# Correcting a list scheduler's estimate of the first weight and input transfers in a one-core Trainium2 encoder layer

## The chip, the cores and the metric

The kernel runs on one NeuronCore of a Trainium2 chip. Its engines are TensorE (PE in the profile; its weight loads are shown apart as PEld), ScalarE (ACT), VectorE (DVE), GpSimd (POOL) and SyncE (SP, which here does little but issue transfers). Each engine works through its own queue in order and waits on semaphores for what the others deliver. The metric is the device time of one execution in microseconds (us); less is better.

## The reference

One encoder layer over 512 tokens of width 1024, batch 1. The part at which the change works is the very beginning, the projection `h @ w_in`, of which the first 128 columns of keys and the first 256 of queries are computed first. `h` is x (DEPTH is 1); the lines left out put heads in shape and rotate q and k, the two mixers are attention within |i-j| <= 128 with 4 key heads and 16 query heads, and attention at three dilations, merged:

```python
    for l in range(DEPTH):
        proj = h @ w_in[l]
        qa, ka, va, qb, kb, vb = jnp.split(proj, SPLITS, axis=-1)
        ...
        o_a = windowed_gqa_sink(qa, ka, va, a_sink[l]).astype(h.dtype)
        o_b = dilated_mixture(qb, kb, vb).astype(h.dtype)
        gates = jax.nn.sigmoid(h @ w_gate[l] + b_gate[l])
        g_a, g_b = jnp.split(gates, N_BRANCH, axis=-1)
        mixed = g_a * (o_a @ w_br_a[l]) + g_b * (o_b @ w_br_b[l])
        y = mixed @ w_out[l]
        h = layer_norm(DN_ALPHA * h + y, ln1_g[l], ln1_b[l])
        f = (jax.nn.silu(h @ w_ff_gate[l]) * (h @ w_ff_up[l])) @ w_ff_down[l]
        h = layer_norm(DN_ALPHA * h + f, ln2_g[l], ln2_b[l])
```

## The kernel before

**Every product is three matmuls.** Each float32 operand is split into a rounded high part (float32r) and the rest, which the high part leaves. A product is high x high, low x high and high x low, added up in one PSUM bank. So an operand that has been loaded needs two more steps before TensorE can use it: a copy that rounds (on ACT or DVE), and a subtraction on DVE for the rest.

**The first stretch.** x lies as eight tiles of 128 x 512, one for each 128 input channels. Three weight units are multiplied with them together: `k` (the first key tile), `q` and `r` (the first and the second query tile). Each unit comes as two halves of 128 x 512 (four input channel tiles each); the first halves are cut in two pieces of 256 columns (`CUTS`, line 61), and the first piece serves x's first two tiles. `k`'s first piece is loaded over ACT's queue (line 374), everything else over SP's (lines 341 and 378). Copies are issued through line 333 (ACT) and 335 (DVE), the subtractions at lines 382 (weights) and 430 (x). The matmuls of this stretch are single operations at line 941, 72 in all: for each tile of x, nine, listed as high x high for k, q, r, then weight rest x x high for k, q, r, then weight high x x rest for k, q, r (the last two tiles go unit by unit). Ahead of it TensorE is kept busy with eight matmuls on zeros (`spin`, line 407).

**The order is written by a planner.** The kernel is built as a list of operations with dependencies, a priority, and for each engine that may do it a cost. `Program.run` (line 171) plays a clock over them: whenever an engine is free, it takes the ready operation with the best priority whose buffers fit, and that is the order in which the instructions of that engine are written into its queue. What is ready when, is the planner's own estimate. It is not a time of the chip: the chip executes the written order, whatever its own times are.

- A transfer by SP occupies SP for 0.45 (0.62 where it is small, cost up to 0.2). `dma[1]` is the time at which the transfer engines have moved all that was issued so far; a transfer adds its cost to it, 0.73 for 256 KB, and has landed 0.9 later (lines 242 to 244). One that another engine issues adds `moves` and has landed 2.0 later (lines 246 to 248). Both start from `dma = [0.0, 0.0]` (line 178).
- A result is seen by another engine after a hop of 0.20, by TensorE after 0.33, by the same engine after 0.11 (line 47).
- A copy may go to ACT or DVE. DVE takes one only if ACT isn't free within the next 0.2 (`BIAS`, line 220).
- A buffer is free again 0.20 after its last user. There are six buffers for weights on their way in (`ws`); the halves of k, q and r take all six.
- Priorities of the first operations are fixed in `FIRST` (line 62), the smaller the earlier: -1000 for k's first piece, -999.9 for x's first tile, -999.7 for q's and -999.6 for r's first piece. Constants (cosine, sine, mask, sink, identity) have about -95, the gate bias -119, the weights of the next units about -114 and more.

```python
                        if o.ready <= now and (best is None or o.prio < best.prio) and self.fits(o):
                            if e == DVE and len(o.alts) > 1 and free[ACT] < now + BIAS:
                                continue
                            best = o
```

**After it** comes the order of line 74: the next query unit `q2` (lines 454 to 456), the values `VA` (lines 627 to 629), the rotation `T`, gates `G` between the attention units `A0` to `A3` (transposes at line 675, which wait for the normalising copy at line 663), and so on to the feed-forward part, whose products are taken by a seven-product scheme (lines 1312 to 1314, 1441 to 1443).

Of the kernel before, what the change touches and what calls it, by code (L numbers as in the profile page):

```python
# [16 lines left out]
S = 512  # L17
# [28 lines left out]
PE, ACT, DVE, POOL, SP = "PE", "ACT", "DVE", "POOL", "SP"  # L46
# [11 lines left out]
D_BANK = "s"  # L58
SPIN = 4

CUTS = ((0, 256), (256, 512))
FIRST = {("k", 0): (-1000, -998.4), ("q", 0): (-999.7, -998.2), ("r", 0): (-999.6, -998.1),
         ("k", 1): (-997.7,), ("q", 1): (-997.5,), ("r", 1): (-997.4,),
# [34 lines left out]
class Program:  # L98
# [16 lines left out]
    def op(self, alts, fn, reads=(), writes=(), prio=0.0, after=(), abs_prio=None, moves=0.0):  # L115
        o = Op()
        o.urgent = self.urgent
        o.alts, o.fn = alts, fn
        o.prio = (self.T + prio if abs_prio is None else abs_prio, len(self.ops))
        o.ready, o.done, o.eng = 0.0, None, None  # L120
        deps = set(a for a in after if a is not None)
        for t in reads:
            deps.update(self.writer.get(t, ()))
        for t in writes:
            deps.update(self.writer.get(t, ()))
            deps.update(self.readers.get(t, ()))
        deps.discard(o)
        for t in reads:
            self.readers.setdefault(t, []).append(o)
        for t in writes:  # L130
            self.writer[t] = [o]
            self.readers[t] = []
        o.bufs, o.new = [], []
        o.strict, o.moves = self.strict, moves
        for t in list(reads) + list(writes):
            b = self.buf_of(t)
            if b not in o.bufs:
                o.bufs.append(b)
                b.users += 1
        o.succ = []  # L140
        o.left = len(deps)
        for d in deps:
            d.succ.append(o)
        self.ops.append(o)
        return o
# [25 lines left out]
    def run(self):  # L171
# [2 lines left out]
        pending = {e: [] for e in engines}  # L174
        times = [0.0]
        frees = []
        dma = [0.0, 0.0]

        def add(o):
            heapq.heappush(times, o.ready)  # L180
# [99 lines left out]
def dve(n, fast=False, extra=0.0):  # L280
    return 0.069 + (0.00074 if fast else 0.00104) * n + extra
# [7 lines left out]
def hybrid_layer(ctx: ExitStack, tc: tile.TileContext, wpack, xT, xtok, sink, bgate,  # L289
                 ln1g, ln1b, ln2g, ln2b, ropec, ropes, maska, maskb, identd, out):  # L290
    nc = tc.nc
# [9 lines left out]
    op = pr.op  # L301
# [7 lines left out]
    def slot(dt=F32, cls=None):  # L309
        cls = cls or "gen"  # L310
        return Buf("slot", cls, lambda: slab.tile([P, S], dt, tag="slab", bufs=N_SLOT, name=name("sl")))
# [19 lines left out]
    def copy(eng, dst, src):  # L331
        if eng == ACT:
            nc.scalar.activation(dst, src, AF.Copy)  # L333
        else:
            nc.vector.tensor_copy(dst, src)

    def f32(ap):
        return ap.bitcast(F32)
# [5 lines left out]
    def cp_alts(n, ps=False):  # L344
        return [(ACT, act(n, ps)), (DVE, dve(n, not ps))]
# [21 lines left out]
    def half_unit_by(u, j, cuts, prios):  # L367

        st, h, l = slot(F32, "ws"), slot(F32R, "whl"), slot(F32R, "whl")
        pieces[h] = pieces[l] = cuts  # L370
        for (c0, c1), ap in zip(cuts, prios):
            w = c1 - c0
            if ap == -1000:
                op([(ACT, 0.4)], lambda e, c0=c0, c1=c1: nc.scalar.dma_start(
                    st.t[:, c0:c1], wpack[u, :, j * S + c0:j * S + c1]), writes=[(st, c0)], abs_prio=ap,
                   moves=0.73 * w / S)
            else:
                op([(SP, 0.73 * w / S)], lambda e, c0=c0, c1=c1: nc.sync.dma_start(
                    st.t[:, c0:c1], wpack[u, :, j * S + c0:j * S + c1]), writes=[(st, c0)], abs_prio=ap)
            op(cp_alts(w), lambda e, c0=c0, c1=c1: copy(e, h.t[:, c0:c1], st.t[:, c0:c1]),  # L380
               reads=[(st, c0)], writes=[(h, c0), (l, "room", c0)], abs_prio=ap)
            op([(DVE, dve(w))], lambda e, c0=c0, c1=c1: nc.vector.tensor_tensor(
                l.t[:, c0:c1], st.t[:, c0:c1], f32(h.t[:, c0:c1]), op=ALU.subtract),
               reads=[(st, c0), (h, c0)], writes=[(l, c0)], abs_prio=ap)
        return h, l
# [36 lines left out]
    for j in range(2):  # L422
        for w, u in (("k", U_KA), ("q", U_QA), ("r", U_QA + 1)):
            first[w, j] = half_unit_by(u, j, ((0, S),) if j else CUTS, FIRST[w, j])
    for j in range(KD):
        st, ap = slot(F32, "xs"), FIRST["x"][j]
# [1173 lines left out]
```

## Time and profile before

| | before |
|---|---|
| median of 3 runs | 779.84 us |
| lowest and highest | 779.28, 780.75 us |
| profiled execution, whole | 779.7 us |
| its span, first to last instruction | 777.9 us |
| mean granted TensorE clock | 0.997 |
| instructions in the span | 13378 |

The profile is of one execution. Its span runs from the first to the last instruction; all instants below are counted from its start. In a row of the timeline stand start, duration, engine, line and operation, what is written and read, how many instructions are merged in the row, and in brackets how long the engine stood idle before and what ended that. A row of waits reads: who waited, for whom, total us, times, longest. A row of the windows view gives for a stretch its length, then for PE, PEld, DVE, ACT and POOL the busy time and the number of instructions, then granted clock, share of the DMA engines and GB/s. Issues of transfers are rows of "SPq" or "ACTq". Matmuls overlap: the duration of a 512-column matmul is 0.39, though one follows the other at 0.23.

### The profile page before, as it was taken

Reading aid. Unit: us, or ns where it says so; the run is one execution under the profiler, and the core shown is the slowest. Engines: PE = TensorE matmul, PEld = TensorE weight load, DVE = VectorE, ACT = ScalarE, POOL = GpSimd, SP = SyncE. Lnnn points to the kernel's source line nnn. Section 1 sums busy time; section 2 is a strip of 40 time slices with the busy share of each in tenths; the row PEclk is TensorE's granted clock in tenths of the full one; section 3 lists DMA queues with packets and bytes.
Section 4 is the critical chain, followed back from the end, with each engine's and each line's share of the span. In section 5 each row is a group of like instructions: output and inputs, shape, how many; then the busy total and the mean of one; then the engine's idle time right before and its main releaser. Section 6 shows DMA issues by size and latency. Waiting matters only on the chain.

```text
span 777.9 us, 13378 instructions
## 1 busy us (share of the span) xinstructions
PE 766.2 (99%) x4470; PEld 675.9 (87%) x4470; DVE 652.7 (84%) x1373; ACT 479.7 (62%) x1057; POOL 122.2 (16%) x288
## 2 busy tenths in 40 slices
PE   8999999999999999999999999999999999999995
PEld 6888888888888888888888899999999999999984
DVE  6378999888989898696686999797988889888697
ACT  6257785778787688693341767556655566555631
POOL 0011010101005204200020010232102331122002
PEclk9999999999999999999999999999999999999998
DMA  8745232203223224354472497699867987789102
GB/s 274 211 138 196 79 105 82 90 28 110 83 87 102 81 86 153 109 183 141 136 208 63 116 245 221 142 200 203 222 188 161 228 184 212 179 214 216 43 1 108
DMA packets 68848, 113.35 MB, mean 146 GB/s; under 512 B 8620, under 2 KB 17068, under 8 KB 68780
## 3 DMA queue, kind: packets, MB, share of 16 engines
q1 hardware_dynamic: 57116, 91.40, 36.4%
q0 software_dynamic: 11520, 20.98, 16.5%
q8 instruction: 35, 0.57, 0.3%
q14 instruction: 33, 0.27, 0.1%
q10 hardware_dynamic: 144, 0.13, 0.1%
HBM read 104.87 MB, written 4.72 MB: 141 GB/s over the span
## 4 chain that ended last, share of the span: by engine, by line
PE 96%; DVE 1%; ACT 1%; DMA 1%; issue 0%; SPq 0%; DVEq 0%; ACTq 0%
PE ps L454 10%; PE ps L455 10%; PE ps L456 10%; PE ps L1314 9%; PE ps L1313 9%; PE ps L1312 9%; PE ps L1441 4%; PE ps L1442 4%; PE ps L1443 4%; PE ps L675 3%; PE ps L1077 3%; PE ps L1079 3%; PE ps L1078 3%; PE ps L941 2%; PE ps L627 2%; PE ps L629 2%
## 5 line engine op out<-in xcount | busy, mean ns | idle before, releaser
L333 ACT ACTIVATE sl<-sl 128x512 fp32r<-128x512 f32 (+4 forms) x456 | 247.9, 571 | 79.7 <-DMA sl<-wpack 20.4
L1196 DVE TENSOR_TENSOR sl<-sl,sl 128x512 fp32r<-128x512 f32 (+3 forms) x304 | 169.8, 602 | 11.2 <-ACT sl L333 7.2
L333 ACT ACTIVATE sl<-ps 128x256 f32<-128x256 f32 (+4 forms) x188 | 81.6, 450 | 106.3 <-PE ps L1314 65.6
L454 PE MATMUL ps<-x,sl 128*128 128x512 f32 x280 | 110.9, 396 | 0.0
L455 PE MATMUL ps<-x,sl 128*128 128x512 f32 x280 | 109.5, 391 | 0.0
L456 PE MATMUL ps<-x,sl 128*128 128x512 f32 x280 | 109.3, 390 | 0.0
L354 DVE TENSOR_TENSOR sl<-sl,sl 128x512 fp32r<-128x512 f32 x114 | 75.5, 685 | 8.8 <-ACT sl L333 7.8
L1266 POOL DMA_DIRECT2D sl<-wpack x44 | 40.7, 1008 | 267.1 <-DMA sl<-wpack 144.1
L1312 PE MATMUL ps<-x,sl 128*128 128x256 f32 x264 | 74.8, 283 | 0.0
L1314 PE MATMUL ps<-x,sl 128*128 128x256 f32 x264 | 74.7, 283 | 0.0
L1313 PE MATMUL ps<-x,sl 128*128 128x256 f32 x264 | 74.7, 283 | 0.0
L1196 DVE TENSOR_TENSOR sl<-sl,ps 128x512 f32<-128x512 f32 (+1 forms) x78 | 47.3, 610 | 25.4 <-PE ps L1314 16.2
L456 PEld LDWEIGHTS ps<-x,sl 128*128 128x128 f32 x280 | 52.6, 188 | 11.5
L454 PEld LDWEIGHTS ps<-x,sl 128*128 128x128 f32 x280 | 52.7, 188 | 8.5
L455 PEld LDWEIGHTS ps<-x,sl 128*128 128x128 f32 x280 | 52.7, 188 | 8.3
L1313 PEld LDWEIGHTS ps<-x,sl 128*128 128x128 f32 x264 | 50.6, 192 | 0.5
L1312 PEld LDWEIGHTS ps<-x,sl 128*128 128x128 f32 x264 | 50.6, 192 | 0.5
L1314 PEld LDWEIGHTS ps<-x,sl 128*128 128x128 f32 x264 | 50.6, 192 | 0.0
L1314 PE MATMUL ps<-tw,sl 128*128 128x256 f32 x176 | 49.8, 283 | 0.0
L1313 PE MATMUL ps<-tw,sl 128*128 128x256 f32 x176 | 49.8, 283 | 0.0
L1314 PE MATMUL ps<-sl,sl 128*128 128x256 f32 x176 | 49.8, 283 | 0.0
L1313 PE MATMUL ps<-sl,sl 128*128 128x256 f32 x176 | 49.8, 283 | 0.0
(151 smaller groups left out, 1891.9 us busy)
## 6 DMA issues: line engine op xcount, KB each, us to landing
sl<-wpack SPq DMA_DIRECT2D x235, 256.0 KB, 3.7
sl<-wpack POOLq DMA_DIRECT2D x44, 256.0 KB, 5.6
wf<-wpack SPq DMA_DIRECT2D x36, 256.0 KB, 5.3
wf<-wpack POOLq DMA_DIRECT2D x36, 256.0 KB, 6.8
sl<-sl SPq DMA_DIRECT2D x88, 32.0 KB, 1.9
sl<-wpack SPq DMA_DIRECT2D x21, 128.0 KB, 4.3
sl<-xT SPq DMA_DIRECT2D x8, 256.0 KB
sl<-xtok SPq DMA_DIRECT2D x8, 256.0 KB, 2.9
```

What stands on the lines that cost most here:

```text
L333: nc.scalar.activation(dst, src, AF.Copy)
L354: op([(DVE, dve(S))], lambda e: nc.vector.tensor_tensor(l.t, src.t, f32(h.t), op=ALU.subtract), reads=[src, h], writes=[l], prio=prio, abs ...
L454: mm(o, a, x0, start=(k == 0), stop=False)
L455: mm(o, a, x1, start=False, stop=False)
L456: mm(o, b, x0, start=False, stop=(k == nk - 1))
L1196: op([(DVE, dve(w))], lambda e: nc.vector.tensor_tensor(dst(), x(), y(), op=o), reads=reads, writes=writes, prio=prio)
L1266: return op([(POOL, 1.0)], lambda e: nc.gpsimd.dma_start(dst.t, wpack[u, :, j * S:(j + 1) * S], accum_op=ALU.add), reads=[dst], writes=[ds ...
L1312: mm(o, wh, bh[k](), start=(first and k == 0), stop=False, skip_group_check=True)
L1313: mm(o, wh, bl[k](), start=False, stop=False, skip_group_check=True)
L1314: mm(o, wl, bh[k](), start=False, stop=(k == 3), skip_group_check=True)
L1441: mm(ps.t, x0, w[0].t, start=(first and m == 0), stop=False, skip_group_check=True)
L1442: mm(ps.t, x0, w[1].t, start=False, stop=False, skip_group_check=True)
```

## The change

The planner's account of the first transfers is changed in two places, and nothing else. The clock of the transfer engines starts at 2.2 instead of 0. And the load with priority -999.6, which is the first piece of `r`, costs 1.8 more in the account; as `dma[1]` runs on, every later transfer stands 1.8 later in it too. No operation, buffer, priority or cost of an engine is changed; which instructions are written stays, their order in each queue is what the planner makes of the new account. All lines behind line 60 stand one lower in the new code.

```diff
 SPIN = 4
 
+SLOW = -999.6
 CUTS = ((0, 256), (256, 512))
...
-        dma = [0.0, 0.0]
+        dma = [0.0, 2.2]
...
             else:
-                op([(SP, 0.73 * w / S)], lambda e, c0=c0, c1=c1: nc.sync.dma_start(
+                op([(SP, 0.73 * w / S + 1.8 * (ap == SLOW))], lambda e, c0=c0, c1=c1: nc.sync.dma_start(
                     st.t[:, c0:c1], wpack[u, :, j * S + c0:j * S + c1]), writes=[(st, c0)], abs_prio=ap)
```

## The prediction

> **What bounds the kernel now.** I read the page's busy times first, then who waited for whom on TensorE, then the chain that ended last, then the rows of the first ten microseconds, engine by engine. The page says at once which engine to look at: TensorE (PE) is busy for 99% of the span and holds 96% of the chain.
>
> ```profile
> PE 766.2 (99%) x4470; PEld 675.9 (87%) x4470; DVE 652.7 (84%) x1373; ACT 479.7 (62%) x1057; POOL 122.2 (16%) x288
> PE 96%; DVE 1%; ACT 1%; DMA 1%; issue 0%; SPq 0%; DVEq 0%; ACTq 0%
> ```
>
> So time is won only where PE stands still. The waits of PE over the whole span are three:
>
> ```profile
> PE ps L941 <- ACT sl L333: 1.2, 1, 1.2
> PE ps L409 <- DVE eps L441: 1.2, 1, 1.2
> PE ps L675 <- ACT sl L663: 0.9, 1, 0.9
> ```
>
> The second is the wait for the first spin matmul. The first is the one that the change is about, and the chain shows what is behind it: one weight load, issued by SP at 1.20 after x's first tile, is on its way from 1.65 for 4.82 us, ScalarE (ACT) copies it, and PE goes on.
>
> ```profile
> 0.75 0.39 SPq L341
> 1.20 0.42 SPq L378
> 1.65 4.82 DMA sl<-wpack
> 6.49 0.42 ACT sl L333
> 6.96 16.17 PE ps L941 x70
> ```
>
> The 70 matmuls behind it run without a gap. Of the 72 at L941 only two come before it, so the third in PE's queue, the one of the second q tile ("r" in the code) with x's first tile, holds up those behind it that need only k, q and x (x0 to x7 below are x's eight tiles; x's "rest" is what its rounded high part leaves). PE's rows:
>
> ```profile
> 1.20 3.59 PE L409 MATMUL ps<-warm 128*128 128x512 bf16 x8 [1.20 <-DVE eps L441]
> 4.82 0.92 PE L941 MATMUL ps<-x,sl 128*128 128x512 f32 x2
> 6.96 0.73 PE L941 MATMUL ps<-x,sl 128*128 128x512 f32 x2 [1.23 <-ACT sl L333]
> 8.69 0.62 PE L941 MATMUL ps<-x,sl 128*128 128x512 f32 x2
> 22.97 0.39 PE L454 MATMUL ps<-x,sl 128*128 128x512 f32 x1
> 25.01 0.39 PE L454 MATMUL ps<-x,sl 128*128 128x512 f32 x1
> ```
>
> The last two rows are nine matmuls apart, so one costs (25.01 - 22.97) / 9 = 0.227 us. The row of 8.69 begins with the first matmul of x's second tile: seven matmuls lie between 6.96 and 8.69 (0.34 for the first after a stop, then six at 0.23).
>
> **What the planner will write.** No instruction is added or removed; lines 178 and 379 change the planner's clock, and by it the order of each engine's queue. I work its arithmetic by hand, for the order alone. In the kernel before it thinks that k lands at 2.77, x0 at 2.73, q at 3.10 and r at 3.46, while spin holds PE until 4.07: all is there, so it takes k, q, r as they are listed. With 2.2 in the account: k's load 2.2 + 0.365 + 2.0 = 4.565; x0 (2.565 + 0.73) + 0.9 = 4.195; q 3.66 + 0.9 = 4.56; r (3.66 + 0.365 + 1.8) + 0.9 = 6.725; x1 6.555 + 0.9 = 7.455. The trace puts the copies that wait for x0, k, r and x1 at 4.15, 4.35, 6.49 and 7.17:
>
> ```profile
> 4.35 0.72 ACT L333 ACTIVATE sl<-sl 128x256 fp32r<-128x256 f32 x2 [1.89 <-DMA sl<-wpack]
> 6.49 0.42 ACT L333 ACTIVATE sl<-sl 128x256 fp32r<-128x256 f32 x1 [1.43 <-DMA sl<-wpack]
> 7.17 0.63 ACT L333 ACTIVATE x<-sl 128x512 fp32r<-128x512 f32 x1 [0.26 <-DMA sl<-xT]
> 4.15 0.43 DVE L335 CAST x<-sl 128x512 fp32r<-128x512 f32 x1 [3.00 <-DMA sl<-xT]
> 4.79 0.43 DVE L382 TENSOR_TENSOR sl<-sl,sl 128x256 fp32r<-128x256 f32 x1 [0.21 <-ACT sl L333]
> 5.14 0.68 DVE L430 TENSOR_TENSOR x<-sl,x 128x512 fp32r<-128x512 f32 x1
> 6.94 0.42 DVE L382 TENSOR_TENSOR sl<-sl,sl 128x256 fp32r<-128x256 f32 x1 [0.79 <-ACT sl L333]
> 7.84 0.69 DVE L430 TENSOR_TENSOR x<-sl,x 128x512 fp32r<-128x512 f32 x1 [0.47 <-ACT x L333]
> ```
>
> From these arrivals, with a hop of 0.20: q's copy is ready for ACT at 4.760, k's at 4.765, so ACT takes q first (until 5.067). VectorE (DVE) ends x0's copy at 4.843 and, since ACT is not free before 4.843 + 0.2, line 220 lets it take k's copy, then x0's rest, k's rest, q's rest. PE's queue becomes: q and k with x0's high part, k and q with x0's rest, k's and q's rest with x0's high part, and only then r's three. That is two matmuls ahead of r's copy as now, and four more.
>
> **The sum for PE.** Do the four fit before 6.96? I add durations end to end. The row of ACT's two copies puts the second from about 4.67 to 5.07, so q had landed by then and its copy ends by 5.07 even so. k's copy on DVE (half of the 0.43 row at best, all of it at worst) ends by 5.01. The first two matmuls start by 5.12 and 5.55. On DVE x0's rest ends by 5.01 + 0.68 = 5.69, k's rest by 6.12, q's rest by 6.55; the four matmuls start by 5.78, 6.01, 6.24 and 6.60, the last is through by 6.83, under 6.96. r's copy does not move (SP issues in the same order up to x's last tile), so r's first matmul starts at 6.96, the next at 7.30 as in the row, the third at 7.53; its rest, subtracted from 6.94 to 7.36, is there. The slot behind is 7.76, but x1's copy ends at 7.17 + 0.63 = 7.80, and PE follows ACT by 0.05 (6.49 + 0.42 = 6.91, start 6.96): 7.85. So 0.09 of a new wait, and x's second tile starts at 7.85 where it was 8.69: **0.84 us won**. The idle 1.23 can't all be won: x1's copy is the next thing late. If only two of the four fit, it is 2 x 0.227 = 0.45.
>
> **Does the rest follow?** A tile of x is nine matmuls, 2.04 us, so the tiles now start at 7.85, 9.89, 13.97 (fifth) and 20.09 (eighth). What each needs:
>
> ```profile
> 9.49 0.75 DVE L382 TENSOR_TENSOR sl<-sl,sl 128x256 fp32r<-128x256 f32 x2
> 12.27 1.35 DVE L382 TENSOR_TENSOR sl<-sl,sl 128x512 fp32r<-128x512 f32 x2
> 13.60 2.06 DVE L430 TENSOR_TENSOR x<-sl,x 128x512 fp32r<-128x512 f32 x3
> 15.71 1.47 DVE L354 TENSOR_TENSOR sl<-sl,sl 128x512 fp32r<-128x512 f32 x2
> 29.21 0.68 DVE L615 TENSOR_TENSOR sl<-sl,sl 128x512 fp32r<-128x512 f32 x1
> ```
>
> x1's rest is there at 8.53 and used from 7.85 + 6 x 0.227 = 9.21. r's second piece is ready at 10.24, used at 9.89 + 5 x 0.227 = 11.02; r's second half at 13.62, used at 15.10; x7's rest at 15.66, used after 20. The margins are 0.7 us and more.
>
> One thing moves that the change doesn't name. The planner now frees k's staging buffer at about 9.5 of its clock instead of before 7, while SP is free at 7.8, so SP is given what needs no such buffer: cosine, mask, sine and sink go ahead of the next q unit's weights, which came right behind the gate bias.
>
> ```profile
> 9.61 0.35 SPq L341 DMA_DIRECT2D bg<-bgate  x1
> 14.29 0.80 SPq L341 DMA_DIRECT2D sl<-ropec  x1
> 17.14 0.47 SPq L341 DMA_DIRECT2D sl<-maska  x1
> 17.65 0.66 SPq L341 DMA_DIRECT2D sl<-ropes  x1
> 18.35 0.45 SPq L341 DMA_DIRECT2D nsink<-sink  x1
> ```
>
> These issues add 0.80 + 0.47 + 0.66 + 0.45 = 2.4 us to what waits behind them on SP's queue. The next q unit's weights are split by 15.71 + 1.47 = 17.18 and used at 22.97, soon 22.13: 4.9 us of cover, less 2.4. The value unit's last weights are split at 29.89, used four further tiles after it starts; they stand behind these constants either way. I cost this at nothing; without the cover it is up to 2.4.
>
> Behind that PE has, by the three rows of its waits, none until the transposes at 328 us, so an earlier PE carries its 0.84 to the end, provided that the planner's later order stays. Its clock for PE shifts by about 2.4 us as a whole (x1 starts at 8.5 instead of 6.1), which shifts no choice by itself, and the two engines that prepare operands have much idle time in which differences die out:
>
> ```profile
> 20.00:40.00 20.00, 20.00 (x90) 16.55 (x89) 8.57 (x15) 4.76 (x8) 0.00 (x0) 1.00 0.67 198
> ```
>
> DVE is busy for 8.57 us of these 20, ACT for 4.76. **Sum:** the profiled execution took 779.7 us (span 777.9 and 1.8 around it); 779.7 - 0.84 = 778.9. The median of the three timed runs is 779.84, 0.14 above it, so 779.84 - 0.84 = 779.0. The three runs spread from 779.28 to 780.75, 0.19%; 0.2% (1.56 us) is about what a measurement of this kernel can tell from no change, and 0.84 is 0.11%.
>
> [...] The row of 4.82 shows two matmuls in 0.92 us and the spin before it 3.59 / 8 = 0.45 each, against 0.227 later: PE comes to full speed at about 5.3. [...]
>
> **Rivals.**
> Half the gain: DVE's order costs more than I added, two of the four fit; 779.4. For it: the first two matmuls can now start 0.3 later than 4.82. Against: the margin of 0.13 in a sum of worst cases. Chance 0.08.
> Nothing to win: r's long flight of 4.82 is of the profiled execution alone. Then the idle isn't in the timed runs, and either order takes the same: 779.84. No view of one execution excludes it. Chance 0.09.
> Slower: the planner's choices hang on near ties (4.760 against 4.765; ACT free at 5.067 against 5.043), and PE's queue is strictly in order. If later ones flip too, the transposes between 60 and 330 us are where it shows: one already stands ahead of ACT's normalising, for 0.86 us.
>
> ```profile
> 328.74 0.55 PE L675 MATMUL ps<-ident,sl 128*128 128x128 f32 x3 [0.86 <-ACT sl L663]
> ```
>
> One more such wait cancels the gain, three more make 779.0 + 2.6 = 781.6, slower by 0.23%; it decides from three. For it: almost no wait is left to lose, many could come. Against: the idle time of DVE and ACT above. Chance 0.10, and 0.05 for one or two.
> [...] Chance 0.04.
> Faster: the same reshuffling takes away the 0.86 at L675: 779.0 - 0.86 = 778.1. Chance 0.08.
> The change does nothing: the equality in line 379 fails, or PE's order stays; 779.84. The same literal stands on both sides, so 0.01.
>
> **How the numbers follow.** The forecast has 0.55: 779.0. Range 778.2 to 780.6: from just above the faster case, over the half gain, no gain, the late gate and one or two new waits; left out are the three waits and part of the faster case. Faster by over 0.2% (under 778.28) is the 0.08 and some 0.07 of the forecast, by the spread of the runs: 0.15. Slower by over 0.2% (above 781.40) is the 0.10 and 0.02 for a weight unit late beyond its cover: 0.12. Within 0.2%: 0.73.
>
> **What would show it.** Right: six matmuls of L941 (a line lower in the new code) before the one that follows r's copy, an idle of 0.1 to 0.4 us there instead of 1.23, x's second tile at 7.8 to 7.9, q before k on ACT, ropec issued before the next weights, the value unit some 0.84 earlier, one wait at the transposes. Wrong: a new wait of PE between 8 and 60 us (a margin misjudged), several at the transposes (the third rival), or the same 1.23.

## The result, and the profile after

| | before | after |
|---|---|---|
| median | 779.93 us (16 runs) | 781.22 us (16 runs) |
| lowest and highest | 779.09, 780.92 | 780.63, 784.28 |
| ratio of the runs, 95% interval | | 1.0021 [1.0013, 1.0029] |
| profiled execution, whole | 779.7 | 780.9 |
| its span | 777.9 | 778.7 |

The changed kernel is slower by 1.3 us. The forecast was 779.0 in a range from 778.2 to 780.6.

The waits of TensorE (PE) in the changed kernel. Its lines are one higher than before's: L942 is the line of the first products, L455 to L457 are those of every later unit, L676 is the transposes.

```profile
PE ps L676 <- ACT sl L664: 0.9, 1, 0.9
PE ps L942 <- ACT x L334: 0.6, 1, 0.6
PE ps L457 <- DVE sl L355: 0.5, 1, 0.5
PE ps L455 <- ACT sl L334: 0.3, 1, 0.3
PE ps L942 <- ACT sl L334: 0.2, 1, 0.2
```

The 1.2 at the first products has become 0.6 + 0.2. The wait at the transposes is as it was. New are two waits at L455 and L457. PE's rows at both places (start, length, then line, tiles and count):

```profile
4.89 2.68 PE L942 MATMUL ps<-x,sl 128*128 128x512 f32 x9 [0.19 <-ACT sl L334]
8.14 14.58 PE L942 MATMUL ps<-x,sl 128*128 128x512 f32 x63 [0.58 <-ACT x L334]
28.00 0.39 PE L628 MATMUL ps<-sl,x 128*128 128x512 f32 x1
...
49.53 0.39 PE L630 MATMUL ps<-sl,x 128*128 128x512 f32 x1
50.26 0.50 PE L455 MATMUL ps<-x,sl 128*128 128x512 f32 x1 [0.34 <-ACT sl L334]
...
51.51 0.50 PE L457 MATMUL ps<-x,sl 128*128 128x512 f32 x1 [0.52 <-DVE sl L355]
```

And the same places before:

```profile
28.41 0.39 PE L627 MATMUL ps<-sl,x 128*128 128x512 f32 x1
...
50.62 0.39 PE L456 MATMUL ps<-x,sl 128*128 128x512 f32 x1
```

The value unit starts at 28.00 instead of 28.41: 0.41 won at the start. It has no gap, so the unit behind it, the first gate unit, could begin at 49.53 + 0.23 = 49.76. It begins at 50.26, and its third matmul stands again. The stop is 1.45 us in all: from the value unit's first matmul to the 156th behind it (95 more of its own, then 61 that follow it) takes 63.14 - 28.41 = 34.73 before and 64.18 - 28.00 = 36.18 after. From there to the last matmul both need the same 706.3 us (769.45 - 63.14, 770.53 - 64.18). So in the profiles 1.45 - 0.41 = 1.04 us are lost. This reading, **start of the value unit, stop at the gate unit, 706.3 us**, is made of every kernel below.

Why do the gate unit's weights come late? Followed back in the changed kernel: TensorE waits for the subtraction (DVE L355), that for the rounding copy (ACT, 128x512), which stands in ACT's queue behind the casts of the rotated heads (64x512); the casts wait for the rotated rows to come back (SP L505), those for the rotation (DVE L495), and that for the copies that SP writes for it (L484). Rows of the changed kernel:

```profile
34.07 1.15 SPq L484 DMA_DIRECT2D sl<-sl  x2
38.24 0.01 DVE L495 LOAD_MASK_SELECT sl<-sl  x1 [6.67 <-DMA sl<-wpack]
43.09 1.29 ACT L334 ACTIVATE sl<-sl 64x512 fp32r<-64x512 f32 x2 [8.85 <-DMA sl<-sl]
49.58 3.24 ACT L334 ACTIVATE sl<-sl 128x512 fp32r<-128x512 f32 x6
50.74 3.73 DVE L355 TENSOR_TENSOR sl<-sl,sl 128x512 fp32r<-128x512 f32 x6
```

Of the kernel before:

```profile
32.80 1.14 SPq L483 DMA_DIRECT2D sl<-sl  x2
36.95 0.01 DVE L494 LOAD_MASK_SELECT sl<-sl  x1 [7.05 <-DMA sl<-wpack]
41.81 1.28 ACT L333 ACTIVATE sl<-sl 64x512 fp32r<-64x512 f32 x2 [7.17 <-DMA sl<-sl]
48.31 3.24 ACT L333 ACTIVATE sl<-sl 128x512 fp32r<-128x512 f32 x6
49.44 3.70 DVE L354 TENSOR_TENSOR sl<-sl,sl 128x512 fp32r<-128x512 f32 x6
```

The rotation's rows name a weight load as what ended the wait, because it shares a semaphore with SP's copies (in the changed kernel the load issued at 35.26 with the copy issued at 30.55). The last of these copies landed at 37.73, and at 36.38 before. Every link is 1.27 to 1.30 us later. Before, the first subtraction of this row ended at 50.13 and was used at 50.62: **about 0.5 us of slack, on a chain of which no wait of TensorE told.**

And why is SP late? The constants now come ahead, as the prediction said. SP's rows of the changed kernel:

```profile
10.56 0.81 SPq L342 DMA_DIRECT2D sl<-ropec  x1
11.42 0.41 SPq L342 DMA_DIRECT2D sl<-maska  x1
11.87 0.67 SPq L342 DMA_DIRECT2D sl<-ropes  x1
...
13.20 0.34 SPq L342 DMA_DIRECT2D sl<-wpack  x1
14.31 0.33 SPq L342 DMA_DIRECT2D ident<-identd  x1
15.45 0.33 SPq L342 DMA_DIRECT2D sl<-wpack  x1
15.83 1.24 SPq L611 DMA_DIRECT2D sl<-wpack  x2
17.63 0.34 SPq L342 DMA_DIRECT2D sl<-maskb  x1
19.29 7.01 SPq L611 DMA_DIRECT2D sl<-wpack  x12
```

From the gate bias to the end of the rotation's copies SP issues the same 38 transfers in both kernels, in another order. That takes 24.3 us before (9.61 to 33.94) and 25.3 after (9.90 to 35.22). A merged row also holds the waits between its transfers. Taken one by one, the issues add up to 19.2 us before and 19.4 after, the time between them to 5.1 and 5.9. So SP is hardly busier; it stands 0.8 us more, and 0.3 of the 1.27 were lost at the gate bias already, ahead of the constants. Its waits for constants up to 36 us, after and then before:

```profile
SPq L611 <- DMA sl<-ropes: 1.3, 1, 1.3
SPq L342 <- DMA sl<-maska: 0.6, 1, 0.6
SPq L611 <- DMA sl<-ropec: 0.4, 1, 0.4
```

```profile
SPq L341 <- DMA sl<-ropec: 1.4, 1, 1.4
```

That is 2.3 us for constants instead of 1.4. From the gate bias on SP also stands 0.5 us more for x's tiles, and 0.6 less for weights.

In both traces, up to 26 us, SP issues a load only when the one eight places earlier has landed. In the changed kernel ropec, maska and ropes are the first three rows behind the gate bias, and the loads that wait for them are the ninth to eleventh. Sine, issued at 11.87, landed at about 19.27. In the trace each of these issues itself waits for one of eight semaphores, which the loads raise in turn; so the wait stands in the program.

### The profile page after: what moved, and what is told of

The parts are those of the page before. It is cut to its first block, busy times and chain, and to the rows that moved or that the text cites. A ratio compares the mean times of both kernels' runs of the same rounds, so it can differ in the third digit from the quotient of the medians.

```text
span 778.7 us, 13366 instructions
## 1 busy us (share of the span) xinstructions
PE 766.9 (98%) x4470; PEld 675.5 (87%) x4470; DVE 653.0 (84%) x1374; ACT 480.0 (62%) x1056; POOL 123.0 (16%) x288
## 4 chain that ended last, share of the span: by engine, by line
PE 91%; DMA 4%; ACT 2%; DVE 2%; SPq 1%; issue 0%; DVEq 0%; ACTq 0%
PE ps L457 10%; PE ps L455 10%; PE ps L456 10%; PE ps L1315 9%; PE ps L1314 9%; PE ps L1313 9%; PE ps L1442 4%; PE ps L1443 4%; PE ps L1444 4%; PE ps L676 3%; PE ps L1080 3%; PE ps L1079 3%; PE ps L1078 3%; DMA sl<-wpack 2%; ACT sl L334 2%; PE ps L578 1%
## 5 line engine op out<-in xcount | busy, mean ns | idle before, releaser
L334 ACT ACTIVATE sl<-sl 128x512 fp32r<-128x512 f32 (+3 forms) x455 | 247.6, 572 | 79.8 <-PE ps L456 20.3
L455 PE MATMUL ps<-x,sl 128*128 128x512 f32 x280 | 111.0, 397 | 0.3 <-ACT sl L334 0.3
L457 PE MATMUL ps<-x,sl 128*128 128x512 f32 x280 | 109.4, 391 | 0.5 <-DVE sl L355 0.5
L355 DVE TENSOR_TENSOR sl<-sl,sl 128x512 fp32r<-128x512 f32 x114 | 75.5, 686 | 8.8 <-ACT sl L334 7.9
L457 PEld LDWEIGHTS ps<-x,sl 128*128 128x128 f32 x280 | 52.6, 188 | 12.4 <-DVE sl L355 0.9
L455 PEld LDWEIGHTS ps<-x,sl 128*128 128x128 f32 x280 | 52.7, 188 | 9.2 <-ACT sl L334 0.8
```

The lines of the kernel that those rows point to most:

```text
L355: op([(DVE, dve(S))], lambda e: nc.vector.tensor_tensor(l.t, src.t, f32(h.t), op=ALU.subtract), reads=[src, h], writes=[l], prio=prio, abs ...
L455: mm(o, a, x0, start=(k == 0), stop=False)
L457: mm(o, b, x0, start=False, stop=(k == nk - 1))
```

## The experiments

One row for each kernel, from its profile and its timed runs beside runs of the kernel before on the same chip (medians 779.65 to 779.72 there). "VA" is the start of the value unit, "stop" what the 156 matmuls behind take over 34.73, "last" the start of the last matmul.

| kernel | VA | stop | last | median | ratio, 95% |
|---|---|---|---|---|---|
| before | 28.41 | 0 | 769.45 | 779.93 | |
| after | 28.00 | 1.45 | 770.53 | 781.22 | 1.0021 [1.0013, 1.0029] |
| e1 start only | 28.08 | 1.84 | 770.98 | 780.58 | 1.0010 [1.0001, 1.0018] |
| e2 r only | 27.30 | 2.30 | 770.62 | 780.48 | 1.0006 [0.9997, 1.0014] |
| e3 constants held | 27.70 | 0.63 | 769.42 | 779.27 | 0.9988 [0.9979, 0.9997] |
| e4 before, constants first | 28.05 | 0.80 | 769.88 | 780.77 | 1.0015 [1.0006, 1.0024] |
| e5 constants by ACT | 28.09 | 1.49 | 770.68 | 779.88 | 1.0003 [0.9994, 1.0012] |
| e6 order alone | 27.40 | 0.68 | 769.12 | 779.61 | 0.9999 [0.9991, 1.0008] |
| e7 two more buffers | 27.68 | 0 | 772.27 | 782.71 | 1.0040 [1.0028, 1.0053] |
| e8 e6, turn first | 27.60 | 0 | 768.61 | 779.06 | 0.9992 [0.9983, 1.0001] |
| e9 after, turn first | 27.55 | 1.63 | 770.30 | 780.60 | 1.0009 [1.0000, 1.0018] |
| e10 after, by GpSimd | 30.77 | 0 | 771.92 | 782.52 | 1.0041 [1.0028, 1.0053] |
| e11 e6, by GpSimd | 32.75 | 0 | 773.91 | 783.77 | 1.0054 [1.0041, 1.0066] |
| e12 after, by GpSimd, held | 27.98 | 0 | 769.22 | 778.82 | 0.9988 [0.9979, 0.9997] |
| e13 e6, by GpSimd, held | 27.55 | 0.31 | 769.12 | 779.36 | 0.9995 [0.9986, 1.0005] |
| e14 e13, turn first | 27.49 | 0.01 | 768.64 | 778.49 | 0.9986 [0.9978, 0.9995] |

But for e7, the last matmul starts 706.3 to 706.5 us after that 156th in every one. A profile is one execution: e4's median is 0.7 further from before's than its profile says, and the profiled executions of e1 (781.3) and e5 (780.8) were 0.7 and 0.9 over their medians. Where an interval contains 1, as for e2, e5, e6, e8 and e13 (e9's begins there), the time can't be told from before's, and only the profile speaks.

**e1 and e2: each half of the change.** e1 has only `dma = [0.0, 2.2]`, e2 only the 1.8 on r's load. e1:

```diff
-        dma = [0.0, 0.0]
+        dma = [0.0, 2.2]
```

> Only the first half of the change: the transfer clock starts at 2.2, no 1.8 for r's first piece. The planner then takes q, k, r for x's first tile (r third again) and gives SP ropec, then the first half of the next q unit's weights, then maska, the second half, two value loads, ropes, and so on: the constants are mixed with the weights, where the changed kernel has all four ahead. Theory A (the constants ahead of the weights on SP's queue delay the rotation, whose casts stand ahead of the first gate unit's weight copies on ACT, so that PE waits when it comes to that unit): the first gate unit starts later than 50.2 us and PE waits there for 0.3 to 1.2 us; PE still stands before r in x's first tile where r lands late; 780.0 to 781.0 us. Rival B (the loss comes from the new order of x's first tile): that order is not there, so 779.9 us and no wait at the gate unit.

> Only the second half of the change: r's first piece costs 1.8 more, the transfer clock starts at 0. PE's order in x's first tile is k and q, then r, as in the changed kernel; on SP ropec, half a weight unit, maska, the other half, two value loads, ropes, sink. Theory A: as in the run with the other half, a wait of PE at the first gate unit of 0.3 to 1.2 us, less the 0.4 to 0.8 won at the start; 779.5 to 780.8 us. Rival B (the order of x's first tile costs): 781.2 us with or without a wait at the gate unit.

Both medians lie in the range of theory A, and either half brings the stop by itself, 1.84 and 2.30. e1 keeps r third and gains little at the start; e2 gains most there (1.1 us, no idle at all) and loses twice that at the gate unit. The place of the loss is thus not where the gain is.

**e3 and e4: the constants' place, with the new order and with the old.** In e3 the changed kernel's constants are held behind the value unit's first loads; e4 is the kernel before with the constants' priority raised above the next q unit's weights.

```diff
# e3, on the changed kernel
+    def constants():
+        load(cosT, ropec[0:16].unsqueeze(0).broadcast_to([8, 16, S]), abs_prio=-108.3, after=[va_loads[0]])
+        load(mA, maska, abs_prio=-108.3, dst=lambda: mA.t[:, :384], after=[va_loads[1]])
...
# e4, on the kernel before
-    for t_, src, ap in ((cosT, ropec, -95.3), (sinT, ropes, -95.2)):
+    for t_, src, ap in ((cosT, ropec, -118.4), (sinT, ropes, -118.2)):
...
```

> The changed kernel with the constants held back in the planner: cosine, mask A, sine, sink and identity are issued after the next q unit's weights and the first four of the value unit's eight weight tiles, nearly as in the kernel before. PE's order of x's first tile stays that of the changed kernel. Theory A: the rotation starts at 37.0 us or earlier, no wait of more than 0.2 us at the first gate unit, the 0.4 to 0.84 us of the start arrive at the end: 779.1 to 779.5 us, 0.05 to 0.1% under the kernel before. Rival B (the order at the start costs): still 781.2 us.

> The kernel before with one thing changed: cosine, mask A, sine and sink have a priority that puts them right behind the gate bias, ahead of the next q unit's weights. PE's order of x's first tile is that of the kernel before. Theory A: the value unit's loads and the rotation come about 1.3 us later, PE waits at the first gate unit for 0.5 to 1.5 us: 780.5 to 781.4 us, 0.1 to 0.2% over the kernel before, without anything won at the start. Rival B: 779.9 us as before, since PE's order is unchanged and the constants have cover.

e3 has the changed kernel's order on TensorE and is faster than before; its stop is 0.63. e4 has the old order, idles before r as before does, and is slower by 0.15%; a stop of 0.80 appears in its profile. The rotation starts at 37.17 in e3 and at 38.24 in the changed kernel; with the old order it starts at 37.70 in e4 and at 36.95 before. Both medians came as theory A expected, though e3 kept a wait of 0.33 where at most 0.2 was expected. So the new order of TensorE costs nothing; the constants' place does.

**e6: the order alone.** r's three matmuls of x's first tile are made to follow the six of k and q in the kernel before, which are now listed unit by unit; SP's order stays.

```diff
-        for (wp, xp), (w, ps) in ([(p, w) for p in parts for w in ws] if k < 6 else [(p, w) for w in ws for p in parts]):
+        for (wp, xp), (w, ps) in ([(p, w) for p in parts for w in ws] if 0 < k < 6 else [(p, w) for w in ws for p in parts]):
...
+                   after=kq if w == "r" and k == 0 else ())
+            if k == 0 and w != "r":
+                kq.append(o)
```

> The kernel before with nothing but the order of x's first tile changed: r's three matmuls depend, for the planner alone, on the six of k and q. Account, SP's and DVE's orders are those of the kernel before. Theory A: the start wins what r's late landing cost, 0.3 to 0.8 us by how late r lands in that execution, the rotation starts at about 37 us as before, and as the first gate unit's weights are ready only 0.5 us ahead of use in the kernel before, 0 to 0.3 us of the gain is lost there again: 779.0 to 779.5 us, 0.03 to 0.09% faster. Rival B (the order itself costs): 781 us. Rival C (r's landing of 6.49 was of one execution, so there is nothing to win): 779.7 us.

The value unit starts 1.01 us earlier, and 0.68 of that is given back at the gate unit: the weights come when SP's chain lets them, and TensorE, earlier, now meets it. More is lost than the 0 to 0.3 that was expected. That is the slack of 0.5 seen from the other side. No difference from before can be measured.

**e5: the constants on another queue.** In the changed kernel, ACT issues four of them behind its copy of x's last tile (identity and the second mask stay on SP).

```diff
+        op([(ACT, 0.4)], lambda e: nc.scalar.dma_start(dst() if dst else b.t, src), writes=[b], abs_prio=ap,
+           after=[xload], moves=mb)
```

> The changed kernel with cosine, mask A, sine and sink loaded over ACT's queue, behind x's last copy, instead of SP's; identity and mask B stay on SP, ahead of the next q unit's weights. The same bytes move in the same stretch; SP has four issues less and nothing of these four among the loads whose landing it waits for. Theory A1 (SP's queue is what counts: its issue time, and its waits for loads issued eight places earlier): the value unit's last load is issued 2 us or more before 28.2, the rotation starts by 36.5, no wait of PE at the first gate unit, 778.9 to 779.4 us. Theory A2 (the bytes ahead of the weights count, whoever issues them): the rotation stays at 37.5 to 38.5 us, PE waits at the gate unit for 0.5 us or more, 780.0 us or more.

SP still waits for them, though ACT issued them (at 16.89 and later), and the stop stays, 1.49:

```profile
SPq L614 <- DMA sl<-ropec: 1.6, 1, 1.6
...
SPq L614 <- DMA sl<-ropes: 1.1, 1, 1.1
```

The eight places count the loads of both queues. The rotation (38.41) and the stop are those of the second expectation, the time lies between the two; as SP stood for these landings all the same, the run doesn't part them.

**e7: two more weight buffers.** `N_WHL` 18 instead of 16, so that the gate unit's first half is copied before the casts.

> The changed kernel with two more buffers for split weights (18 instead of 16, two fewer general ones), so that the planner copies the first half of the first gate unit's weights ahead of the rotation's casts on ACT. SP's order stays as in the changed kernel, the rotation stays late, at about 38.2 us. Theory A's last link (the weight copies stand behind the casts on ACT): no wait of PE at the first gate unit, the start's gain gets through, 779.0 to 779.8 us if the later order costs nothing; the buffers change the later order, which can cost 1 us or more, so the wait is the test, not the time. If the wait at the gate unit stays at 0.5 us or more although its copies come early, the last link is wrong.

That copy moves from behind the casts to ahead of them, and the stop is gone, with the rotation as late as in the changed kernel (38.37): the last link of the chain is right. ACT's rows:

```profile
32.48 0.63 ACT L333 ACTIVATE sl<-sl 128x512 fp32r<-128x512 f32 x1 [1.17 <-DMA sl<-wpack]
...
43.25 1.29 ACT L333 ACTIVATE sl<-sl 64x512 fp32r<-64x512 f32 x2 [9.33 <-DMA sl<-sl]
```

The planner's later order changes with the buffers and costs more elsewhere (1.5 at one later unit), so this is no remedy.

**e8 and e9: SP's order before the rotation.** The last two copies for the rotation are issued ahead of the four or five weight loads that SP has before them; the planned order of the other engines is kept. In `run`:

```diff
...
+                    if o is self.raws[3]:
+                        for fn in [q.fn for q in self.turns[6:8]] + later:
+                            fn(SP)
...
```

> The kernel of the run with the order alone, in which the second q unit's two copies for the rotation (the last of the turn's writes, at 32.32 us there) are issued as soon as their source is copied, ahead of the four weight loads that SP has before them; the planned order on all other engines is left as it is. Theory (the first gate unit's weights wait behind the rotation, and the rotation behind SP): four loads at about 0.52 us each let these writes start near 30.2 us, the rotation near 34.8 (36.87), and the gate unit's weight copies on ACT 1.0 to 2.0 us earlier (48.24); the stop of TensorE at the gate unit, 0.6 us there, is gone. The time is then 0.3 to 0.6 us under that kernel's: 779.0 to 779.3 us beside 779.7 of the kernel before. Rival (the rest after the gate unit holds the time anyway, or the weight loads that now come later are late themselves): a new wait of 0.3 us or more shows at the gate unit or behind it, and the time stays at 779.6 or over.

> The changed kernel with the same edit: the second q unit's two copies for the rotation ahead of the five weight loads that SP has before them (they start at 34.07 us in the changed kernel, 32.80 in the one before); the constants stay ahead of the value unit's weights, and TensorE keeps its new order at the start. Theory: five loads at about 0.52 us make it near 31.5, the rotation starts near 35.6 (38.24), and the stop of 1.4 us at the gate unit goes: 779.4 to 780.0 us. Rival (the changed order of TensorE itself, or the constants' place, costs the time in another way): the rotation comes earlier as said and the time stays at 780.8 to 781.3.

e8 came out as expected, with no stop; its rotation starts at 33.32, where e6's starts at 36.87. **e9 was a miss:** the rotation starts 3.4 us earlier than in the changed kernel (34.86), and the casts don't (43.01). e9's rows:

```profile
34.86 0.01 DVE L501 LOAD_MASK_SELECT sl<-sl  x1 [2.85 <-DMA sl<-sl]
38.43 5.29 SPq L511 DMA_DIRECT2D sl<-sl  x8
43.01 1.29 ACT L340 ACTIVATE sl<-sl 64x512 fp32r<-64x512 f32 x2 [9.22 <-DMA sl<-sl]
```

The first rotated rows leave at 38.43, 3.6 us after the rotation's start instead of 2.8, because SP is still issuing other copies. They are used 4.6 us later, where it took 2.0 before (39.79 to 41.81). On their way they share the DMA engines with the six weight loads that SP issues from 33.25 on. e9 from 37 to 40 us, and then the kernel before from 40 to 43 us, when its rotated rows are on their way (columns: the stretch and its length, busy time and instructions of PE, PEld, DVE, ACT and POOL, the granted clock, the busy share of the DMA engines, GB/s):

```profile
37.00:40.00 3.00, 3.00 (x15) 2.48 (x14) 0.68 (x1) 0.00 (x0) 0.00 (x0) 1.00 0.93 299
```

```profile
40.00:43.00 3.00, 3.00 (x15) 2.49 (x14) 0.99 (x3) 1.16 (x2) 0.00 (x0) 1.00 0.15 36
```

That the sharing slows them fits e8 too, where they take 4.3 us (36.17 to 40.45); no run shows it alone. My chain was too narrow: not the rotation's start alone, but all that SP has to get moved by then, is late. SP had stood for cosine and sine in e9, 3.4 us:

```profile
SPq L617 <- DMA sl<-ropes: 2.2, 1, 2.2
...
SPq L617 <- DMA sl<-ropec: 1.2, 1, 1.2
```

The changed kernel also moves less, most of all from 13 to 16 us. Before, then after:

```profile
13.00:16.00 3.00, 3.00 (x15) 2.49 (x14) 2.94 (x5) 2.65 (x5) 0.00 (x0) 1.00 1.10 355
```

```profile
13.00:16.00 3.00, 3.00 (x15) 2.45 (x15) 2.26 (x4) 1.99 (x4) 0.00 (x0) 1.00 0.76 203
```

The DMA engines are not full there after. SP starts four issues in this stretch in both kernels, and what it stands for in the changed one is x's last two tiles (1.6 us), not a constant; so the two rows show that less is moved, not why. Summed over the seven such rows from 10 to 31 us, the changed kernel has moved 5.0 MB and the one before 5.5; the missing 0.45 MB are 1.3 us at 355 GB/s.

**e10 and e11: the constants by GpSimd.** Five constants go to GpSimd's queue, meant to follow x's last tile.

```diff
+        op([(POOL, 1.0)], lambda e: nc.gpsimd.dma_start(dst() if dst else b.t, src), writes=[b], abs_prio=ap,
+           moves=0.73, after=xlast)
```

> The changed kernel with cosine, sine, mask, sink and identity issued by GpSimd's queue behind the copy of x's last tile, so that SP issues five loads fewer and none of them is one on whose landing SP waits eight places later, if loads of another queue don't count. Theory in its two forms. Landing (SP's loss is its standing for the constants' landings, 1.6 us more between 9.9 and 35.2 us than before): the waits for cosine, sine and mask are gone from SP's list, the turn's last writes start 1.6 us and the five issues of 2.6 us earlier, near 30 us, and the gate unit's stop is gone: 779.2 to 780.0 us. Counting across queues (as the run with ACT's queue showed for cosine, 1.6, and sine, 1.1): SP still stands some 2.5 us for these landings, the writes start near 32.5, and the time is 779.6 to 780.4. Rival (the order of TensorE): 780.8 to 781.3 in both.

> The kernel of the run with the order alone, with the five constants issued by GpSimd's queue in the same way. Theory: the turn's last writes start 2 to 3 us earlier than 32.32, the rotation 1.5 to 3 us earlier than 36.87, the 0.6 us at the gate unit go, and the time is 779.0 to 779.3. Rival (identity, cosine or mask land later than the value unit, the rotation or the first attention need them, by the slower queue): a wait for one of them shows on DVE or TensorE and the time is 779.7 or over.

Both missed the time: the dependency holds in the planner's clock only, nothing on the chip makes GpSimd wait, and the constants left at 1.28, among x's tiles, which then came late (e10: waits of 1.9 for x, value unit at 30.77). The value unit starts 2.8 us later than in the changed kernel, and e11's 5.4 later than e6's: that is the price of these bytes in front of x (in e11 with a granted clock of 0.50 from 12 to 14 us, shown at the end). Yet SP has no wait for a constant in either, and there is no stop at the gate unit, so GpSimd's loads don't count among the eight. The 1.6 us in e10's expectation takes the waits inside merged rows for issues; one by one they are the 0.8 above.

**e12 to e14: held.** GpSimd first copies one column of x's last tile, so its loads follow that tile's landing.

```diff
+    xlast[:] = [op([(POOL, 0.1)], lambda e: nc.gpsimd.tensor_copy(mark.t, st.t[:, 0:1]), reads=[st], writes=[mark],
+                   abs_prio=-999)]
```

> The changed kernel with the five constants issued by GpSimd's queue, and GpSimd kept by a copy of one column of x's last tile from issuing them before that tile has landed: the constants' bytes move at about the time they do in the changed kernel (from 10 us), and none of their landings is one that SP waits for. If SP's standing is the loss: SP has no wait for cosine, sine or mask, the turn's last writes start at 32 us or before (34.07), the rotation at 36.9 or before (38.24), and the stop at the first gate unit (1.4 us) is gone or under 0.5: 779.3 to 780.2 us. If the bytes ahead of the weights are the loss: the weights land as late as before, the rotation starts at 37.8 or later, and the time is 780.6 to 781.4.

> The kernel with the order alone, with the five constants on GpSimd's queue behind x's last tile in the same way. By SP's standing: SP loses 2.6 us of issue and about 1 us of waits before the turn's last writes, so that these start near 30 (32.32 in the run with the order alone), the rotation near 34.5 to 35.5 (36.87), and the 0.6 us at the gate unit go: 778.9 to 779.3 us, beside 779.6 of the order alone. By the bytes: the constants now move earlier than in the run with the order alone, the value unit's weights land later, and the time is 779.8 to 780.8.

> The last one with the second q unit's copies for the rotation ahead of four weight loads as well. By SP's standing: the rotation starts near 33.5, and as the gate unit no longer waits in the last one either, the time is the same within 0.2 us: 778.8 to 779.3. By the bytes: 779.5 or over, with the gate unit's weights the later ones.

In e12 cosine leaves at 15.15 (not from 10 us, as I had expected; in e5 it was 16.89). SP waits for no constant, the rotation starts at 35.58, the stop is gone:

```profile
15.15 0.82 POOL L438 DMA_DIRECT2D sl<-ropec  x1
31.96 1.14 SPq L490 DMA_DIRECT2D sl<-sl  x2
35.58 0.01 DVE L501 LOAD_MASK_SELECT sl<-sl  x1 [4.68 <-DMA sl<-sl]
```

From 22 to 25 us, e5 and then e12:

```profile
22.00:25.00 3.00, 3.00 (x15) 2.49 (x14) 1.73 (x4) 0.89 (x2) 0.00 (x0) 1.00 0.72 210
```

```profile
22.00:25.00 3.00, 3.00 (x15) 2.49 (x14) 1.81 (x3) 1.57 (x4) 0.00 (x0) 1.00 1.16 227
```

e5 and e12 move nearly the same bytes from nearly the same time on. SP stands in both, but in e12 for no constant; most of it is for weights:

```profile
SPq L617 <- DMA sl<-wpack: 3.7, 4, 2.0
...
SPq L341 <- DMA sl<-wpack: 1.4, 3, 0.8
```

From the gate bias to the end of the rotation's copies SP stands 9.5 us in e5, 2.8 of it for constants, and 8.0 in e12. That is 1.5 of the 1.95 us by which the last two copies start earlier in e12 (33.91, 31.96). In e12 the constants are on their way beside SP's eight loads, in e5 among them: from 22 to 25 us the DMA engines are 1.16 and 0.72 busy, though SP stands about as long there in both (1.9 us for weights, 1.6 for cosine). That speaks for the eight places and the standing that they bring, and against the bytes as such; it is not one thing alone, since ACT stood on its own issues in e5 too and 1.7 us lie between the two starts. Nor is it standing alone against the changed kernel: e12's SP has five issues less (15.3 us of issues instead of 19.4) and stands longer (8.0 instead of 5.9).

e12 is the changed kernel, with the gain at the start kept: 0.12% under before, 2.4 us under the changed kernel's own median, and 0.5 under the lowest that was expected. e14, the fastest, is e6 with the constants held on GpSimd and e8's edit: 778.49. e12 and e14 can't be told apart by their intervals. e13's 779.36 lies between its two expectations, next to the first; its stop of 0.31 shows that the earlier TensorE meets the chain again, which e14's edit cures.

e14 came out 0.3 under what was expected.

What stays open: how the loss divides between SP's standing, the eight places and the order of the bytes, and by how much the waits at the gate unit differ from one execution to the next. The changed kernel's runs spread over 3.7 us, e12's over 1.2. Standing for a constant is not the loss by itself: in e3 SP stands 3.1 us for cosine, sine and mask, more than in the changed kernel, and the rotation starts 1.1 us earlier.

## Why the prediction was wrong

- **The planner's order: right.** TensorE does six matmuls of k and q before r's, ACT takes q's copy and DVE k's, and ropec, maska, ropes and sink stand ahead of the next q unit's weights.
- **"0.84 us won": mis-sized, 0.41.** x's second tile starts at 8.14, not 7.85, because x1's copy began at 7.46 in this execution (7.17 before), and the stop there costs another 0.1: the first matmul behind it takes 0.34 instead of 0.23 (8.14, 8.48), which the sum had counted for r's stop and not for x1's. The second rival was partly right: r's copy began at 6.49 in the profile that I read, at 5.22 in the changed kernel's, 5.98 in e1's and 6.13 in e4's. The 1.8 is one execution's value. The start itself holds more: e2 and e6 won 1.0 to 1.1.
- **"I cost this at nothing": the step that failed.** The two covers that I named held: neither the next q unit nor the value unit waits. But I asked only who needs the loads that the constants are moved past, and not what else stands behind them on SP: the copies for the rotation, and behind these the casts and the gate unit's weights. And the price is not the 2.4 us of issue, which SP pays either way: SP stood 0.8 us more and was 0.3 late at the gate bias already, the rotation started 1.29 later, and TensorE's stop at the gate unit was 1.45. e4, with the old order of TensorE, shows that the constants' place brings it.
- **"So an earlier PE carries its 0.84 to the end": failed with it.** An empty list of TensorE's waits does not mean that there is slack. The gate unit's weights were ready 0.5 us ahead of use, so at most half a microsecond of any gain at the start could pass; e6, with SP's order untouched, shows it.
- **The rivals.** The slower one had the new waits in the wrong place (the transposes, from a reshuffled later order; the later order stayed) and of another kind; its price, 781.6, was near by accident. The point named as what would make the prediction wrong, a new wait of PE between 8 and 60 us from a margin misjudged, is what happened. The range also counts a late gate. No run shows such a term: in the changed kernel the eight matmuls of the spin take 3.51 us, and the first nine behind it, begun at 4.89 instead of 4.82, take 2.68, where nine at the spin's pace would take 3.9 (9 x 3.51 / 8).
- **The forecast's own mechanism** exists where the constants are out of SP's way: e12's median is 0.84 under before's, its profile shows 0.43 of it at the value unit and 0.23 at the last matmul.

## What to carry to other kernels

When a step moves ahead in a queue, follow everything behind it in that queue to its last user, and work out for each user when its operand was ready and when it was used: an engine without a wait may have as little as 0.5 us in hand. A planner's account fitted to one trace also decides what goes first elsewhere, so compare the orders of all queues, and check that a dependency in the planner's clock is also one on the chip.

## What the runs showed of the hardware that was not expected

- SP stands until the load eight places earlier has landed, counted over SP's and ACT's queues (in e5 1.6 us for cosine and 1.1 for sine, which ACT issued), not over GpSimd's (in e10 and e12 no wait for a constant). In the changed kernel's trace the loads of SP and ACT raise eight semaphores in turn (99, 101, 103 to 108) and SP's issues from 4.24 to 25.83 each wait for the one that they raise; GpSimd's loads raise eight others (111 to 118). So the wait is the program's; that the chip asks for it isn't shown. A constant of 256 KB took 7.4 us to land (sine, after, with the DMA engines 0.76 to 1.00 busy), so eight issues of about 0.5 us each don't cover it.
- In e11 TensorE stood 2.0 and 1.15 us between 7 and 11.3 us, and the granted clock fell:

```profile
10.00:11.00 1.00, 0.18 (x1) 0.00 (x0) 0.00 (x0) 0.36 (x1) 0.00 (x0) 1.00 1.08 217
...
12.00:13.00 1.00, 1.00 (x4) 0.81 (x3) 0.42 (x1) 0.68 (x2) 0.00 (x0) 0.50 1.07 380
13.00:14.00 1.00, 1.00 (x3) 0.76 (x3) 0.61 (x1) 0.97 (x3) 0.00 (x0) 0.50 1.05 387
```

It is 0.64 from 11 to 12 us, 0.65 from 14 to 15, and back at 1.00 from 15 us. Between the two stops lie three matmuls (8.98 to 10.17). In e10, whose longest stop there is 1.51 us, it stays at 1.00 in every microsecond from 9 to 15. That the stops brought it down in e11 is a reading of one execution; no run shows it alone.
